# A hybrid decoder layer: the first adaLN weights loaded in two halves of features, with half contractions of two gate tiles and the norm statistics of all chunks between them

## The chip, the cores and the metric

The kernel runs on one core of a Trainium2 chip. The metric is the device time of one execution in microseconds; lower is better. It is one layer of one inference step in float32, launched once.

## The reference

Only the part around the change matters here. Tokens are the columns: 1024 of a prompt and 8 x 4 of samples, 1056 in all; the model has 1024 features, 8 blocks of 128 (called k below).

```python
mod = silu(c) @ w_ada + b_ada      # -> shift1, scale1, gate1, shift2, scale2, gate2
xn  = RMSNorm(x) * (1 + scale1) + shift1
h, B, C, q, k, v, gate_conv, gate_att = split(xn @ w_in)
...
x = x + gate1 * ((sigmoid(gate_conv) * conv_out + sigmoid(gate_att) * attn_out) @ w_o)
```

`w_ada` has 6144 columns; the first 2048 give shift1 and scale1. Behind these lines come a gated convolution, a dilated attention with caches, and an MLP; the change does not touch them.

## The kernel before

The program is a Python class, `Trunk`, that issues the instructions of every engine in an order written out by hand. Each engine works through its own instructions in that order and waits on semaphores where it needs another engine's result.

**Number format.** A float32 product is computed as three passes of a rounded format: each operand is split into a high part (a cast on ScalarE, ACT) and a low part (a subtraction on VectorE, DVE, or GpSimd, POOL), and `gemm` (L365) issues high x high, high x low and low x high for every k: 24 matmuls for a tile of 128 outputs and a chunk of columns. `prep_to` (L185) does this split for a weight tile, `load_to` (L175) loads its raw form into one of 8 weight buffers.

**Chunks and tiles.** The 1056 columns are worked on in 3 chunks of 352 (`CH`). The first four output tiles are gate tiles (w_in tiles 60 to 63), computed with `gemm` by `plain_tiles` (L290): the chunks in turn with tiles 0, 1 and 2, then tile 3. Behind them follow pairs of tiles in a scheme with fewer products (`pair_job`, L243), which needs the products of weights that `products` (L211) makes on ACT and DVE, and sums of the normalised input that `sums` (L325) makes on DVE and POOL.

**The start** (`start`, L429). SP issues the loads in this order: x of chunk 0, `w_ada` for k = 0 to 3, x of chunk 1, `w_ada` for k = 4 to 7, gate weight 0, x of chunk 2, gate weight 1. A load of `w_ada` is a tile of 128 x 1024. Meanwhile:

- `bias_rows` (L604) makes three rows of relative bias on PE and DVE.
- `stats(ch)` (L479) squares the 8 blocks of a chunk on ACT, adds them up on POOL, sums over partitions with a matmul on a matrix of ones, makes the reciprocal root (ACT, then DVE: L387 to L396) and multiplies the 8 blocks by it on DVE (L497). It runs for chunks 0 and 1, with the first four k's of `ada` between them.
- `ada(0)` (L565) computes the 2048 columns as four strips of 32 rows: for each k four matmuls with the same stationary operand (32 columns) at four column positions of the array, each streaming 512 columns. The result is copied, turned by four transposes, and the bias is added; `mod_mul` (L550) makes the scale.
- `apply(ch)` (L501) goes with `modulate` (L398) over the 8 blocks: scale and shift (DVE for even k, ACT for odd k; for chunk 2 two narrow DVE instructions per k besides, L420, for the sample columns), the cast to the high part (ACT) and the low part (DVE for even k, POOL for odd k). Chunk 0 is done at the start.

**Behind the start** a background queue (`bg`) is served in small portions by `slot` (L104) while the gate tiles are issued: `rest` (L509) does `apply(1)`, the statistics of chunk 2 and `apply(2)`; then come `sums` and `bias_spread`. `need` (L137) drains the queue as far as a tile requires. `evac` (L89) copies a finished gate tile out of PSUM, on ACT or DVE in turn.

PSUM banks: three of kind "g", two of kind "s", one each of the others.

Of the kernel before, what the change touches and what calls it, by code (L numbers as in the profile page):

```python
# [17 lines left out]
P = 128  # L18
# [31 lines left out]
class Trunk:  # L50
# [261 lines left out]

    def operand(self, n, k, p):
# [84 lines left out]
    def modulate(self, c, src, r, mul_t, add_t, out, y):  # L398
        nc = self.nc
        n = NPC2 if c == 2 else CH  # L400
        for step in range(KD + 3):
            k = step - 3
            if 0 <= k:
                hi, lo = out(k)
                eng = nc.gpsimd if k % 2 else nc.vector
                eng.tensor_tensor(out=lo, in0=y(k), in1=hi.bitcast(F32), op=ALU.subtract)  # L406
            k = step - 2
            if 0 <= k < KD:
                nc.scalar.copy(out(k)[0], y(k))
            k = step - 1  # L410
            if 0 <= k < KD:
# [11 lines left out]
            if k < KD and r is not None:  # L423
# [5 lines left out]
    def start(self):  # L429
# [20 lines left out]
        wada = self.ada_loads(0, range(4))  # L450
        load_x(1)
        wada.update(self.ada_loads(0, range(4, KD)))
        self.load_to(0)
        load_x(2)
        self.load_to(1)
# [23 lines left out]
        def stats(ch):  # L479
            s = slice(ch * CH, (ch + 1) * CH)  # L480
            acc = None
            for k in range(KD):
                sq = self.chunk("sq")
                nc.scalar.activation(sq, xp[k][:, s], AF.Square)
                if acc is None:
                    acc = sq
                else:
                    nc.gpsimd.tensor_tensor(out=acc, in0=acc, in1=sq, op=ALU.add)
                if k % 2:
                    yield 300  # L490
            ss = self.bank("ada")[:, :CH]
            nc.tensor.matmul(ss, self.ones, acc, start=True, stop=True)
            tmp, r0, r = self.chunk("ln"), self.chunk("r0"), self.chunk("r")
            self.neg_rstd(r, ss, tmp, r0, eps[:, 0:1], 1024 * EPS)
            yield 300
            for k in range(KD):
                nc.vector.tensor_tensor(out=xp[k][:, s], in0=xp[k][:, s], in1=r, op=ALU.mult)  # L497
                if k % 2:
                    yield 300

        def apply(ch):  # L501
            s = slice(ch * CH, (ch + 1) * CH)
            for k, _ in enumerate(self.modulate(ch, None, None, self.mul1, self.add1,
                                                lambda k: (self.xh[k][:, s], self.xl[k][:, s]),
                                                lambda k: xp[k][:, s])):
                if k % 2:
                    yield 300

        def rest():  # L509
            st2 = stats(2)  # L510
            for i, c in enumerate(apply(1)):
                yield c
                if i < KD // 2:
                    yield next(st2)
            self.ready.add(("xn", 1))
            yield None
            yield None
            yield from st2
            yield from apply(2)
            self.ready.add(("xn", 2))  # L520
            nc.scalar.preload_act_table_set("sigmoid_and_others")

        def run(g, n=1 << 30):
            for _ in range(n):
# [1433 lines left out]
```

## Time and profile before

| | |
|---|---|
| median of 3 runs (lowest to highest) | 2165.97 us (2165.32 to 2166.7) |
| the profiled execution | 2163.8 us |
| its span | 2162.0 us |
| mean granted TensorE clock | 0.979 |
| busy: PE, DVE, ACT, POOL | 94%, 65%, 46%, 36% of the span |
| bytes moved | 325.84 MB, mean 151 GB/s |

The profile is of one execution. Its times count from the start of the span, 0 to 2162 us; the execution's own time is 1.8 us more. PE is TensorE's matmul, PEld its weight load, SPq the queue in which SP issues transfers. A granted clock of 1.00 is 2.4 GHz, 0.50 is 1.2 GHz. An entry "[2.54 <-DVE wlo L197]" says that the engine was idle for 2.54 us before the instruction and that DVE's line 197 ended the wait. A float32 matmul without the split shows as two records.

### The profile page before, as it was taken

How to read it: one execution, taken by the hardware profiler on the slowest of the kernel's cores; microseconds unless marked ns; L12 is line 12 of the kernel's file. 1: busy time of each engine (PE TensorE's matmuls, PEld its weight loads, DVE VectorE, ACT ScalarE, POOL GpSimd, SP SyncE). 2: the span in 40 equal slices, each digit the busy share in tenths (PEclk: the TensorE clock that was granted, in tenths of full speed). 3: DMA queues.
4: the chain of work that ended last, by engine and by line, in shares of the span. 5: the costliest groups of instructions: out<-in, count | busy, mean ns of one | idle time of the engine just before them, and what ended most of it. 6: DMA issues, size and time to landing. Idle time of an engine off the chain costs nothing.

```text
span 2162.0 us, 38832 instructions
## 1 busy us (share of the span) xinstructions
PE 2021.7 (94%) x15092; PEld 1907.2 (88%) x15092; DVE 1404.3 (65%) x2935; ACT 989.3 (46%) x2193; POOL 782.6 (36%) x553
## 2 busy tenths in 40 slices
PE   5899999999999999999997989988999999999998
PEld 2799999889899888888886878988999999999998
DVE  4846665435656666556676676378444447999997
ACT  4522223335566556555554322355555556433332
POOL 3645555320111111100011114235233235788785
PEclk8899999999999999999998999999999999999999
DMA  7242221764122445333246774432347729555542
GB/s 284 71 136 62 79 70 35 250 212 148 45 69 74 144 149 167 104 114 116 67 125 199 238 233 145 162 125 88 130 158 274 256 90 350 203 202 198 197 158 102
DMA packets 138096, 325.84 MB, mean 151 GB/s; under 512 B 34232, under 2 KB 77880, under 8 KB 136888
## 3 DMA queue, kind: packets, MB, share of 16 engines
q1 hardware_dynamic: 137480, 323.17, 44.5%
q8 instruction: 118, 1.93, 0.4%
q14 instruction: 66, 0.54, 0.1%
q10 hardware_dynamic: 432, 0.20, 0.0%
HBM read 270.48 MB, written 112.07 MB: 177 GB/s over the span
## 4 chain that ended last, share of the span: by engine, by line
PE 56%; DVE 23%; ACT 5%; issue 3%; DMA 3%; POOL 2%; SPq 0%; DVEq 0%; POOLq 0%; ACTq 0%
PE ps_g L377 23%; DVE acc L1721 5%; DVE wprod L162 5%; PE ps_g L264 4%; PE ps_s L264 4%; PE ps_g L266 4%; PE ps_s L266 4%; PE ps_s L265 4%; PE ps_g L265 4%; DVE hl L1573 1%; DVE wlo L197 1%; ACT S L987 1%; PE ps_o L1015 1%; DVE S L979 1%; PE ps_s L973 1%
## 5 line engine op out<-in xcount | busy, mean ns | idle before, releaser
L162 DVE TENSOR_TENSOR wprod<-wraw,wprod 128x512 fp32r<-128x512 f32 x276 | 270.1, 981 | 173.9 <-ACT wprod L158 173.8
L377 PE MATMUL ps_g<-xh,whi 128*128 128x352 f32 x1056 | 356.6, 338 | 12.8 <-ACT whi L193 6.5
L377 PE MATMUL ps_g<-xh,wlo 128*128 128x352 f32 x1056 | 346.3, 328 | 5.6 <-DVE wlo L197 5.4
L377 PE MATMUL ps_g<-xl,whi 128*128 128x352 f32 x1056 | 346.6, 328 | 3.0 <-POOL xl L406 2.2
L377 PEld LDWEIGHTS ps_g<-xh,whi 128*128 128x128 f32 x1056 | 203.2, 192 | 35.6 <-issue 16.1
L158 ACT CAST wprod<-wraw 128x512 fp32r<-128x512 f32 x276 | 163.3, 618 | 151.0 <-DVE wprod L162 104.1
L377 PEld LDWEIGHTS ps_g<-xl,whi 128*128 128x128 f32 x1056 | 203.9, 193 | 5.9 <-POOL xl L406 4.0
L377 PEld LDWEIGHTS ps_g<-xh,wlo 128*128 128x128 f32 x1056 | 202.7, 192 | 7.2 <-DVE wlo L197 7.2
L197 DVE TENSOR_TENSOR wlo<-wraw,whi 128x512 fp32r<-128x512 f32 x184 | 130.0, 748 | 45.6 <-PE ps_g L377 25.4
L162 POOL TENSOR_TENSOR lo<-qn,hi 128x1024 fp32r<-128x1024 f32 x12 | 33.2, 2770 | 346.7 <-ACT hi L158 346.7
L277 POOL TENSOR_TENSOR ps_z<-ps_z,ps_s 128x264 f32<-128x264 f32 x64 | 60.3, 944 | 252.0 <-DVE ps_s L276 251.8
L264 PE MATMUL ps_s<-th,wprod 128*128 128x264 f32 x512 | 146.3, 286 | 1.7 <-DVE ps_s L276 1.7
L264 PE MATMUL ps_g<-th,wprod 128*128 128x264 f32 x512 | 146.9, 287 | 0.0
L266 PE MATMUL ps_g<-th,wprod 128*128 128x264 f32 x512 | 145.8, 285 | 0.0
L265 PE MATMUL ps_s<-tl,wprod 128*128 128x264 f32 x512 | 145.8, 285 | 0.0
L266 PE MATMUL ps_s<-th,wprod 128*128 128x264 f32 x512 | 145.7, 285 | 0.0
L265 PE MATMUL ps_g<-tl,wprod 128*128 128x264 f32 x512 | 145.5, 284 | 0.0
L987 ACT ACTIVATE S<-S,ng 128x128 f32<-128x128 f32 (+1 forms) x192 | 84.2, 441 | 124.7 <-DVE ng L982 122.8
L193 ACT CAST whi<-wraw 128x512 fp32r<-128x512 f32 x184 | 104.2, 619 | 32.1 <-DMA wraw<-in_w_conv_out 11.4
L264 PE MATMUL ps_g<-xh,wprod 128*128 128x264 f32 x384 | 110.6, 288 | 3.2 <-ACT wprod L158 3.2
L266 PE MATMUL ps_g<-xh,wprod 128*128 128x264 f32 x384 | 110.3, 287 | 3.5 <-DVE wprod L162 3.5
L264 PE MATMUL ps_s<-xh,wprod 128*128 128x264 f32 x384 | 109.9, 286 | 3.4 <-DVE ps_s L280 3.4
(383 smaller groups left out, 6448.3 us busy)
## 6 DMA issues: line engine op xcount, KB each, us to landing
wraw<-in_w_in SPq DMA_DIRECT2D x76, 512.0 KB, 4.1
wada<-in_w_ada SPq DMA_DIRECT2D x48, 512.0 KB, 5.6
hid_d<-hid SPq DMA_DIRECT2D x32, 528.0 KB, 2.9
wraw<-in_w_mlp_in SPq DMA_DIRECT2D x32, 512.0 KB, 6.1
wraw<-in_w_mlp_out SPq DMA_DIRECT2D x32, 512.0 KB, 3.9
hraw<-hid_d SPq DMA_DIRECT2D x56, 264.0 KB, 4.4
kv<-in_v SPq DMA_DIRECT2D x28, 512.0 KB, 5.6
wraw<-in_w_conv_out SPq DMA_DIRECT2D x24, 512.0 KB, 6.7
```

Of the source, the lines that this page charges most:

```text
L158: nc.scalar.copy(hi, src)
L162: eng.tensor_tensor(out=lo, in0=src, in1=hi.bitcast(F32), op=ALU.subtract)
L193: self.nc.scalar.copy(hi[:, s], w[:, s])
L197: self.nc.vector.tensor_tensor(out=lo[:, s], in0=w[:, s], in1=hi[:, s].bitcast(F32), op=ALU.subtract)
L264: nc.tensor.matmul(ps, hi, xh, start=(k == 0), stop=False)
L265: nc.tensor.matmul(ps, hi, xl, start=False, stop=False)
L266: nc.tensor.matmul(ps, lo, xh, start=False, stop=(k == 3))
L277: nc.gpsimd.tensor_tensor(out=z[p], in0=z[p], in1=s[p], op=ALU.add)
L377: self.nc.tensor.matmul(ps, a, x, start=(i == 0), stop=(i == n - 1))
L973: nc.tensor.matmul(ps[hh][:, 256 * i:256 * i + N], q[a][pr, q0:q0 + P], k[b][pr, k0:k0 + N], start=(x == 0), stop=(x == 2))
L987: nc.scalar.activation(s, s, AF.Exp, bias=ng[:, hh, i:i + 1], accum_out=sm[:, hh, i:i + 1])
L1721: nc.vector.tensor_tensor(out=a, in0=a, in1=ps, op=ALU.add)
```

## The change

The `w_ada` loads come in two halves of features. Half f holds the columns of blocks 4f to 4f + 3 of both shift1 and scale1, as tiles of 128 x 2 x 512, one per k. SP's order becomes: x of chunk 0, half 0 (8 loads), gate weight 0, x of chunk 1, gate weight 1, x of chunk 2, half 1 (8 loads), gate weights 2 and 3.

`ada_mm` issues two matmuls (strips f and 2 + f) per k and half. After half 0, blocks 0 to 3 of a chunk can be scaled and shifted, and `first(i, ch, 0)` issues their 12 matmuls, the upper half of the contraction, for gate tiles 0 and 1; the partial sums stay in six PSUM banks. The order is: statistics of chunk 0, weight 0, half 0, `apply(0, 0)`, tile 0; statistics of chunk 1, weight 1, tile 1, `apply(1, 0)`, four k's of half 1, tiles 0 and 1 of chunk 1; statistics of chunk 2, `apply(2, 0)`, the other four k's of half 1, tiles 0 and 1 of chunk 2; the result of half 1, `apply(0, 1)`. `first_tiles` then finishes tiles 0 and 1 chunk by chunk, with `apply(1, 1)` and `apply(2, 1)` from the background queue, and computes tiles 2 and 3 as before. In `stats` the adds are shared: even blocks on POOL, odd ones on DVE, and two matmuls on ones add the two sums.

```diff
--- before.py
+++ after.py
@@ -310,6 +310,30 @@
                 self.wt.pop(base + i)
             self.slot()
 
+    def first_tiles(self, consume):
+        for ch in range(NCH):
+            self.need(("xn", ch))
+            for i in range(2):
+                self.first(i, ch, 1)
+                self.slot()
+                consume(i, ch, self.banks.pop((i, ch)))
+                if ch == 2:
+                    self.wt.pop(i)
+            if ch:
+                self.prep_to(1 + ch, True)
+        for i in range(2, NG):
+            for ch in range(NCH):
+                s = slice(ch * CH, (ch + 1) * CH)
+                ps = self.bank("g")
+                self.gemm(ps[:, :CH], self.wt[i], range(KD), [(self.xh[k][:, s], self.xl[k][:, s]) for k in range(KD)])
+                consume(i, ch, ps)
+                if i == NG - 1:
+                    self.products_to(1 + ch)
+                if i == NG - 2 and ch == 0:
+                    self.load_to(NG)
+                self.slot()
+            self.wt.pop(i)
+
     def operand(self, n, k, p):
         if 2 <= n <= 5:
             i, t = ((0, 0), (1, 1), (0, 1), (1, 0))[n - 2]
@@ -395,20 +419,20 @@
         nc.vector.scalar_tensor_tensor(out=tmp, in0=ss, scalar=eps, in1=tmp, op0=ALU.add, op1=ALU.mult)
         nc.vector.scalar_tensor_tensor(out=out, in0=tmp, scalar=1.5, in1=r0, op0=ALU.subtract, op1=ALU.mult)
 
-    def modulate(self, c, src, r, mul_t, add_t, out, y):
+    def modulate(self, c, src, r, mul_t, add_t, out, y, k0=0, k1=KD):
         nc = self.nc
         n = NPC2 if c == 2 else CH
-        for step in range(KD + 3):
+        for step in range(k0, k1 + 3):
             k = step - 3
-            if 0 <= k:
+            if k0 <= k:
                 hi, lo = out(k)
                 eng = nc.gpsimd if k % 2 else nc.vector
                 eng.tensor_tensor(out=lo, in0=y(k), in1=hi.bitcast(F32), op=ALU.subtract)
             k = step - 2
-            if 0 <= k < KD:
+            if k0 <= k < k1:
                 nc.scalar.copy(out(k)[0], y(k))
             k = step - 1
-            if 0 <= k < KD:
+            if k0 <= k < k1:
                 w = y(k)
                 if k % 2:
                     nc.scalar.activation(w[:, :n], w[:, :n], AF.Identity, bias=add_t[:, k, 0:1], scale=mul_t[:, k, 0:1])
@@ -420,7 +444,7 @@
                         nc.vector.tensor_tensor(
                             out=v, in0=v, in1=tt[:, k, 1:9].unsqueeze(2).to_broadcast([P, NB, NT]), op=op)
             k = step
-            if k < KD and r is not None:
+            if k < k1 and r is not None:
                 nc.vector.tensor_tensor(out=y(k), in0=src(k), in1=r, op=ALU.mult)
             yield
 
@@ -447,12 +471,22 @@
         nc.scalar.dma_start(out=blk, in_=t["blk"])
         self.vec = vec = c.tile([P, 128], F32, name="vec")
         nc.scalar.dma_start(out=vec, in_=t["vec"])
-        wada = self.ada_loads(0, range(4))
+        wada = [[], []]
+
+        def load_ada(f):
+            for k in range(KD):
+                w = self.page("wada", (P, 2, 512))
+                nc.sync.dma_start(
+                    out=w, in_=t["w_ada"][k * P:(k + 1) * P, 0:2048].rearrange("p (a f n) -> p a f n", a=2, f=2)[:, :, f])
+                wada[f].append(w)
+
+        load_ada(0)
+        self.load_to(0)
         load_x(1)
-        wada.update(self.ada_loads(0, range(4, KD)))
-        self.load_to(0)
+        self.load_to(1)
         load_x(2)
-        self.load_to(1)
+        load_ada(1)
+        self.load_to(3)
         self.b_ada, self.g1, self.g2 = vec[:, 0:48], vec[:, 48:56], vec[:, 56:64]
         self.cw = vec[:, 64:88].rearrange("p (a k) -> p a k", a=3)
         eps = c.tile([P, 2], F32, name="eps")
@@ -478,79 +512,123 @@
 
         def stats(ch):
             s = slice(ch * CH, (ch + 1) * CH)
-            acc = None
+            acc = [None, None]
             for k in range(KD):
                 sq = self.chunk("sq")
                 nc.scalar.activation(sq, xp[k][:, s], AF.Square)
-                if acc is None:
-                    acc = sq
+                if acc[k % 2] is None:
+                    acc[k % 2] = sq
                 else:
-                    nc.gpsimd.tensor_tensor(out=acc, in0=acc, in1=sq, op=ALU.add)
-                if k % 2:
-                    yield 300
-            ss = self.bank("ada")[:, :CH]
-            nc.tensor.matmul(ss, self.ones, acc, start=True, stop=True)
+                    eng = nc.vector if k % 2 else nc.gpsimd
+                    eng.tensor_tensor(out=acc[k % 2], in0=acc[k % 2], in1=sq, op=ALU.add)
+            ss = self.bank("pt")[:, :CH]
+            for i in range(2):
+                nc.tensor.matmul(ss, self.ones, acc[i], start=(i == 0), stop=(i == 1))
+            del acc
             tmp, r0, r = self.chunk("ln"), self.chunk("r0"), self.chunk("r")
             self.neg_rstd(r, ss, tmp, r0, eps[:, 0:1], 1024 * EPS)
-            yield 300
             for k in range(KD):
                 nc.vector.tensor_tensor(out=xp[k][:, s], in0=xp[k][:, s], in1=r, op=ALU.mult)
-                if k % 2:
-                    yield 300
-
-        def apply(ch):
+
+        def apply(ch, f):
             s = slice(ch * CH, (ch + 1) * CH)
             for k, _ in enumerate(self.modulate(ch, None, None, self.mul1, self.add1,
                                                 lambda k: (self.xh[k][:, s], self.xl[k][:, s]),
-                                                lambda k: xp[k][:, s])):
+                                                lambda k: xp[k][:, s], 4 * f, 4 * f + 4)):
                 if k % 2:
                     yield 300
 
+        def run(g):
+            for _ in g:
+                pass
+
+        ada_ps = self.bank("ada")
+        ada_m = self.page("ada_m", (P, 512))
+        nc.gpsimd.memset(ada_m, 0.0)
+
+        def ada_mm(f, ks):
+            for k in ks:
+                for c in (f, 2 + f):
+                    nc.tensor.matmul(ada_ps[32 * c:32 * c + 32, :], self.cT[:, k, :], wada[f][k][:, c // 2],
+                                     start=(k == 0), stop=(k == KD - 1), tile_position=(0, 32 * c))
+
+        def ada_out(f):
+            nc.scalar.copy(ada_m[32 * f:32 * f + 32, :], ada_ps[32 * f:32 * f + 32, :])
+            c = 2 + f
+            nc.vector.tensor_copy(ada_m[32 * c:32 * c + 32, :], ada_ps[32 * c:32 * c + 32, :])
+            tr = self.bank("pt")
+            for b in range(4):
+                self.turn(tr[:, b * P:(b + 1) * P], ada_m[:, b * P:(b + 1) * P], self.ident)
+            v = tr.rearrange("p (b c x) -> p c b x", b=4, x=32)
+            for c in (f, 2 + f):
+                nc.vector.tensor_tensor(
+                    out=self.modT[:, 4 * c:4 * c + 4, :], in0=v[:, c, :, 0:9],
+                    in1=self.b_ada[:, 4 * c:4 * c + 4].unsqueeze(2).to_broadcast([P, 4, 9]), op=ALU.add)
+            h = slice(4 * f, 4 * f + 4)
+            self.mod_mul(self.mul1[:, h], 8 + 4 * f, self.g1[:, h])
+
+        def operands():
+            for k in range(4):
+                for v, n in ((self.xh, "xh"), (self.xl, "xl")):
+                    v.append(self.page(n, dt=F32R))
+
+        banks = {}
+
+        def first(i, ch, f):
+            if not f:
+                banks[i, ch] = self.bank("g" if i == 0 else ("s", "ss", "o")[ch])[:, :CH]
+            s = slice(ch * CH, (ch + 1) * CH)
+            hi, lo = self.wt[i]
+            for k in range(4 * f, 4 * f + 4):
+                b = slice(k * P, (k + 1) * P)
+                for x, (a, v) in enumerate(((hi, self.xh), (hi, self.xl), (lo, self.xh))):
+                    nc.tensor.matmul(banks[i, ch], a[:, b], v[k][:, s], start=(k == 0 and x == 0), stop=(k == KD - 1 and x == 2))
+
         def rest():
-            st2 = stats(2)
-            for i, c in enumerate(apply(1)):
-                yield c
-                if i < KD // 2:
-                    yield next(st2)
-            self.ready.add(("xn", 1))
-            yield None
-            yield None
-            yield from st2
-            yield from apply(2)
-            self.ready.add(("xn", 2))
+            for ch in (1, 2):
+                yield from apply(ch, 1)
+                self.ready.add(("xn", ch))
             nc.scalar.preload_act_table_set("sigmoid_and_others")
 
-        def run(g, n=1 << 30):
-            for _ in range(n):
-                if next(g, self) is self:
-                    return
-
         self.bias_rows(*rel)
-        run(stats(0))
-        ada = self.ada(0, wada)
-        run(ada, 1)
-        st1 = stats(1)
-        run(st1)
-        run(ada)
-        self.mod_mul(self.mul1, 8, self.g1)
+        stats(0)
+        self.prep_to(0)
+        ada_mm(0, range(KD))
         self.add1 = self.modT[:, 0:8, :]
-        del wada, ada
-        self.xh = [self.page("xh", dt=F32R) for _ in range(KD)]
-        self.xl = [self.page("xl", dt=F32R) for _ in range(KD)]
-        self.prep_to(0, True)
-        ap0 = apply(0)
-        run(ap0, 1)
-        self.flush_later()
-        run(ap0)
+        ada_out(0)
+        self.xh, self.xl = [], []
+        wada[0] = None
+        operands()
+        run(apply(0, 0))
+        first(0, 0, 0)
+        stats(1)
+        self.prep_to(1)
+        first(1, 0, 0)
+        run(apply(1, 0))
+        ada_mm(1, range(4))
+        first(0, 1, 0)
+        first(1, 1, 0)
+        stats(2)
+        run(apply(2, 0))
+        ada_mm(1, range(4, KD))
+        first(0, 2, 0)
+        first(1, 2, 0)
+        ada_out(1)
+        wada[1] = ada_ps = None
+        del ada_m
+        operands()
+        run(apply(0, 1))
         self.ready.add(("xn", 0))
         self.bg.append(rest())
         self.bg.append(self.sums())
         self.bg.append(self.bias_spread())
+        self.first, self.banks = first, banks
 
     def mod_mul(self, out, t0, g):
         nc = self.nc
-        nc.vector.tensor_scalar(out, self.modT[:, t0:t0 + 8, :], -32.0, -32.0, op0=ALU.mult, op1=ALU.add)
-        nc.vector.tensor_tensor(out=out, in0=out, in1=g.unsqueeze(2).to_broadcast([P, KD, 9]), op=ALU.mult)
+        n = out.shape[1]
+        nc.vector.tensor_scalar(out, self.modT[:, t0:t0 + n, :], -32.0, -32.0, op0=ALU.mult, op1=ALU.add)
+        nc.vector.tensor_tensor(out=out, in0=out, in1=g.unsqueeze(2).to_broadcast([P, n, 9]), op=ALU.mult)
 
     def ada_loads(self, r, ks):
         ws = {}
@@ -562,20 +640,17 @@
                 ws[k, h] = w
         return ws
 
-    def ada(self, r, ws=None):
-        nc = self.nc
-        acc = self.bank("o" if r else "ada")
+    def ada(self, r):
+        nc = self.nc
+        acc = self.bank("o")
         for k in range(KD):
-            if r:
-                ws = None
-                ws = self.ada_loads(r, [k])
-                yield 4
+            ws = None
+            ws = self.ada_loads(r, [k])
+            yield 4
             for c in range(4):
                 nc.tensor.matmul(
                     acc[32 * c:32 * c + 32, :], self.cT[:, k, :], ws[k, c // 2][:, (c % 2) * 512:(c % 2 + 1) * 512],
                     start=(k == 0), stop=(k == KD - 1), tile_position=(0, 32 * c))
-            if k % 4 == 3 and not r:
-                yield 1
         ws = None
         m = self.page("ada_m", (P, 512))
         nc.vector.tensor_copy(m, acc)
@@ -1318,7 +1393,7 @@
         self.rate = 700.0
 
         st = {}
-        self.plain_tiles(0, "xn", lambda i, ch, ps: self.gate(i, ch, ps, st.setdefault(i, {})))
+        self.first_tiles(lambda i, ch, ps: self.gate(i, ch, ps, st.setdefault(i, {})))
         self.last_prod = 7 * sum(len(j) == 2 for j in jobs[NG:])
         ji = NG
         while len(jobs[ji]) == 2:
```

## Rows read from the trace of the kernel before

**Rows 1.** The page, busy us of each engine (share of the span) xinstructions.
```profile
PE 2021.7 (94%) x15092; PEld 1907.2 (88%) x15092; DVE 1404.3 (65%) x2935; ACT 989.3 (46%) x2193; POOL 782.6 (36%) x553
```

**Rows 2.** Windows: stretch, length, each engine's busy us (xinstructions), PEclk, DMA share, GB/s.
```profile
42.64:110.78 68.14, 56.76 (x290) 52.88 (x291) 58.16 (x83) 41.09 (x72) 40.80 (x31) 0.86 0.23 76
0.00:42.64 42.64, 17.33 (x78) 4.00 (x79) 17.44 (x40) 14.71 (x29) 13.81 (x18) 0.90 0.96 346
```

**Rows 3.** Timeline of PE: start, us, engine, line, out<-in, xcount [idle <-releaser].
```profile
17.19 1.54 PE L492 MATMUL ps_s<-sq,ones 128*128 128x352 f32 x2 [2.15 <-POOL sq L488]
18.66 4.71 PE L574 MATMUL ps_s<-wada,cT 128*32 128x512 f32 x32
...
42.64 0.66 PE L377 MATMUL ps_g<-xh,whi 128*128 128x352 f32 x1 [2.11 <-ACT xh L409]
...
110.78 0.28 PE L264 MATMUL ps_g<-xh,wprod 128*128 128x264 f32 x1
```

**Rows 4.** Windows within the gate stage, columns as in rows 2.
```profile
64.00:78.00 14.00, 14.00 (x87) 13.84 (x86) 10.90 (x33) 6.39 (x13) 3.40 (x5) 1.00 0.00 1
96.00:102.00 6.00, 5.34 (x18) 5.34 (x19) 6.00 (x6) 3.75 (x5) 2.98 (x3) 0.50 0.68 212
```

**Rows 5.** Windows of the transfers at the start, columns as in rows 2.
```profile
22.00:24.00 2.00, 1.37 (x16) 0.15 (x8) 2.00 (x5) 1.65 (x4) 0.58 (x1) 1.00 1.08 367
...
28.00:30.00 2.00, 0.00 (x0) 0.00 (x0) 0.24 (x1) 0.00 (x0) 1.92 (x2) 0.50 1.04 416
...
44.00:46.00 2.00, 2.00 (x7) 1.62 (x8) 1.09 (x3) 1.85 (x4) 1.10 (x2) 0.50 0.09 35
```

**Rows 6.** Timeline of PE's weight loads for w_ada, columns as in rows 3.
```profile
19.52 0.20 PEld L574 LDWEIGHTS ps_s<-wada,cT 128*32 128x32 f32 x4 [0.66 <-issue]
20.37 0.20 PEld L574 LDWEIGHTS ps_s<-wada,cT 128*32 128x32 f32 x4 [0.66 <-issue]
...
21.91 0.12 PEld L574 LDWEIGHTS ps_s<-wada,cT 128*32 128x32 f32 x4 [0.31 <-issue]
22.34 0.12 PEld L574 LDWEIGHTS ps_s<-wada,cT 128*32 128x32 f32 x4 [0.31 <-issue]
```

**Rows 7.** Timeline of DVE and POOL from the w_ada result on.
```profile
39.13 0.69 DVE L581 COPY ada_m<-ps_s 128x512 f32<-128x512 f32 x1
...
41.61 0.46 DVE L416 TENSOR_SCALAR x<-x,mul,modT 128x352 f32<-128x352 f32 x1
41.99 1.28 DVE L197 TENSOR_TENSOR wlo<-wraw,whi 128x512 fp32r<-128x512 f32 x2
...
45.78 0.94 POOL L406 TENSOR_TENSOR xl<-x,xh 128x352 fp32r<-128x352 f32 x1 [0.90 <-ACT xh L409]
```

**Rows 8.** Timeline of ACT, POOL and DVE: statistics, of chunk 1 but for the first row.
```profile
10.20 6.94 POOL L488 TENSOR_TENSOR sq<-sq 128x352 f32<-128x352 f32 x7 [9.76 <-ACT sq L484]
...
22.34 3.86 ACT L484 ACTIVATE sq<-x 128x352 f32<-128x352 f32 x8 [1.90 <-DMA x<-in_xT]
...
23.42 7.61 POOL L488 TENSOR_TENSOR sq<-sq 128x352 f32<-128x352 f32 x7 [6.28 <-ACT sq L484]
...
35.65 3.57 DVE L497 TENSOR_TENSOR x<-x,r 128x352 f32<-128x352 f32 x8
```

**Rows 9.** Lines by form, DVE, gate stage: xcount | busy us, mean ns | idle.
```profile
L420 DVE TENSOR_TENSOR x<-x,modT 128x32 f32<-128x32 f32 x8 | 3.5, 431 | 0.3
```

**Rows 10.** Timeline of DVE: the first sums, the first weight product.
```profile
79.35 2.05 DVE L335 TENSOR_TENSOR x<-x 128x528 f32<-128x528 f32 x2
...
106.97 0.68 DVE L162 TENSOR_TENSOR wprod<-wraw,wprod 128x512 fp32r<-128x512 f32 x1
```

**Rows 11.** Timeline of PE: the longest late waits of the gate stage, and one behind it.
```profile
93.20 0.63 PE L377 MATMUL ps_g<-xh,whi 128*128 128x352 f32 x1 [3.34 <-DVE graw L99]
...
96.66 0.66 PE L377 MATMUL ps_g<-xh,wlo 128*128 128x352 f32 x1 [2.54 <-DVE wlo L197]
...
133.04 0.39 PE L264 MATMUL ps_g<-xh,wprod 128*128 128x264 f32 x1 [1.66 <-ACT wprod L158]
```

## Prediction, written before the changed kernel was run

> **What bounds the kernel now.** I read the busy line first: TensorE (PE) is busy 94% of the span [rows 1], so a gain or a loss has to come from time in which PE does not run at its pace. The change touches only the start and the four gate tiles, so the next view is the table by stretches, cut where the first gate matmul and the first paired matmul begin [rows 2, 3]: 42.64 us pass before the first gate matmul, and the gate stage takes 68.14. Undisturbed, PE issues a 352-column matmul every 14.00/87 = 0.161 us at a granted clock of 1.00 (2.4 GHz), and every 5.34/18 = 0.297 us at 0.50 (1.2 GHz) [rows 4]. The stage has 4 tiles x 3 chunks x 24 = 288 matmuls, 46.4 us at the fast pace, so 21.8 us of it are waits and half clock. VectorE (DVE) is busy for 58.16 of the 68.14 us [rows 2]. So there are two prizes: the front, in which PE is nearly idle, and DVE's late work. The change goes for the first.
>
> The front looks bound by transfers: the DMA share is 0.96 [rows 2], and they have ended by 46 us [rows 5]. The reader should ask whether the new order of work keeps up with them.
>
> **The change part by part.** The engines work in program order, so I walk the new order. Times are us from the span's start.
>
> *Transfers.* The same bytes come in another order, with gate weights 2 and 3 sooner; SP issues as many DMAs, and the stores of the bias rows, moved behind more loads, are read only much later. With the second half of w_ada behind x, all has landed by about 46. Its rows are now 2 KB, not 4. The bounds: nothing, and the rate of the stretch in which x (rows of 1.4 KB) arrives, 367 GB/s for 416 [rows 5], on 8.4 MB: 22.9 us for 20.2, +2.7. I take nothing, because the second half is first used after 52 and last after 60 in the walk below; without that cover it costs the 2.7.
>
> *First half of w_ada.* The statistics of chunk 0 end near 18.7 as now [rows 3]: the adds are shared by POOL and DVE, but DVE first does the bias rows, and a second matmul on ones is added. Now 4 k's with four column strips take 4.71 [rows 3]; the weight loads of a pass come in fours, 0.85 apart at the low and 0.43 at the high clock [rows 6]. A k has two passes, so 1.70 or 0.86, with four strips side by side. The change issues two strips per k, hence 16 such steps in place of 8. Bounds for the first 8: 4.7 if a step costs by its matmuls, 13.6 at the low clock; I take 2 x 4.71 = 9.4, since a pass streams the same 512 columns however many strips stand beside it. It ends at 28.1.
>
> By the Trainium skill, "TensorEngine Tiling (Array Packing)", Key Properties, tiles work independently and in parallel; by that rule half the strips save nothing per step, which speaks against this change, and the forecast stands as below, whereas with cost by matmul it would be 4.7 lower. The fours of rows 6 agree with it; no row has a step of two strips.
>
> *First scale and shift.* From the copy of the w_ada result to the first modulation 2.48 pass now [rows 7], so 30.6. The half apply (4 k's): now POOL can start on k = 3 at 45.78, so ScalarE (ACT) is free 4.2 after 41.61, with 1.28 of weight low parts on DVE in between [rows 7]; I take 3.5 to ACT free and 4.5 to the end of POOL's low part. ACT is free at 34.1.
>
> *The link.* ACT reaches the squares of chunk 1 only then. Now its statistics take from 22.34 to 39.22 = 16.9, and POOL's adds end at 31.03 [rows 8]. With the adds shared, the last sum is there 1.0 after the squares (3.86), 4.9 after the start in place of 8.7: -3.8. The second matmul on ones costs +1.2 (0.6 to 1.54, what the present one takes [rows 3]). So a link is 14.3: squares, sums, ones, reciprocal root, 8 normalising instructions. The zero fill of a page on POOL lies in the 9.76 in which POOL has nothing to do [rows 8]; without them it would cost one add, 1.0. Chunk 1 is normalised at 48.4; weight 1's low parts, 1.3 [rows 7], make it 49.7; ACT is free at 53.2, and the low part of k = 3 is there at 54.2.
>
> Chunk 2 would follow at 53.2 + 14.3 = 67.5. But its matmul on ones stands on PE behind 12 matmuls of tile 1 (to 52), four w_ada steps (4.7, to 56.7) and 24 matmuls of the chunk-1 halves (3.9 to 7.1): to 60.6 or 63.8, whereas the sums are ready at 58.1. That is +2.5 to +5.7; I take 2.5, the full clock, since these follow one another closely: 70.0. The half apply has 8 narrow per-sample instructions besides, of 0.43 or less [rows 9] and partly beside other work: 5.2, so 75.2. Then come on PE the last 15 matmuls of the chunk-2 halves, 2.4 to 4.5, taken as 3.4, and behind them the transposes of the second half, with their adds 1.5 (1.8 now [rows 7], with twice as many adds). **The upper half of chunk 0 starts at A = 80.1.**
>
> *What is left on PE.* 72 of 288 matmuls are done. The next 12 go at the pace of the half apply, 5.0; the other 204 x 0.161 = 32.8. For waits behind DVE I take 4, between 0 and 10. The stage ends at 80.1 + 5.0 + 32.8 + 4.0 = 121.9, against 110.78 now [rows 3]: **+11.1**. The second prize is not won either: DVE can start the sums only when all second halves are applied, at A + 4.5 + 4.5 + 5.2 = A + 14.2. From their first instruction to the first weight product 28.3 pass now (79.35 to 107.65 [rows 10]), so the product comes at 122.6. PE and DVE give the same end.
>
> *Behind it* nothing waits on the wall clock: PE goes on at 94%, so the shift stays. The longest such waits now are 3.34 and 2.54 in the gate tiles, and 1.66 for pair weights at 133 [rows 11]; the last may move by a few us either way.
>
> The profiled execution took 2163.8; 2163.8 + 11.1 = 2174.9. The median of the three runs, 2165.97, is 2.2 above it: 2177.
>
> **The rivals.**
> 1. *Everything at its lower end* (no difference). Strips by matmul -4.7, PE's queue -2.5, the 15 matmuls -1.0, waits -4: by PE 2165. DVE does not wait less: A is 71.9, and A + 14.2 + 28.3 = 114.4, +3.6, gives 2170. So 2165 to 2170; that it needs every bound at once speaks against it.
> 2. *The transfers set the front* (faster). Then A is near 50 (landed by 46, last w_ada steps, 2.5 of output), the stage ends at 50 + 41.8 = 92, and the time is 2158 if half of those 19 us are kept, 2147 if all. It decides from A = 110.8 - 41.8 = 69. The DMA share of 0.96 speaks for it. ACT's order speaks against it: 34.1 plus two links is 62.7, with two half applies 71.
> 3. *Half clock through the front* (slower still). Rows 4 and 11 show PE at a granted 0.50 after it had waited; in the new front it works in bursts with waits between. Cost: the first half of w_ada at 13.6 for 9.4, +4.2; four later steps at 6.8 for 4.7, +2.1; 24 matmuls +3.2; 15 matmuls +1.1; in sum 10.6, so 2188. The close queue on PE from 49 to 61 speaks against the middle two.
>
> The Trainium skill, "TensorE: Matmul & The Clock Gate", HAM oscillation, says that bursts with long waits between them each start throttled again. The low clock from 96 to 102, behind two waits, agrees; that is rival 3, with its time.
>
> **How the numbers follow.** Forecast 0.60, rival 1 0.15, rival 2 0.10, rival 3 0.15. A measurement of this kernel tells 0.2%, about 4.3 us, from no change. The forecast and rival 3 are slower by more: 0.75; rival 1 is the same: 0.15; rival 2 is faster: 0.10. The range runs from rival 1's floor, 2165, to rival 3, 2188; it leaves out rival 2 and a tail in which the waits add to rival 3.
>
> **What would show it.** In the changed profile: the first gate matmul near 32, ten us sooner than now; w_ada steps of two strips as long as those of four; ACT idle between the squares of a chunk and its logarithm; the second half of chunk 0's apply at about 80, long after the last w_ada transfer; the first paired matmul near 122, with DVE busy without a break before it. If the upper half starts before 69, the forecast is wrong in sign. If the stage ends at 122 and the total is no longer, something behind it gave the time back, and the wait for pair weights is the place to look.

## The result, and the profile after

The changed kernel takes 2181.57 us (median of 4 runs, 2177.85 to 2183.83) against 2165.7 (median of 4) for the kernel before on the same chip. The ratio is 1.0069, 95% interval 1.0052 to 1.0087: 11 to 19 us slower. The forecast of 2177 had the sign right and the range held the time. But one large term of the sum was missing, and the trace shows it at once.

The page's busy line of the changed kernel, which answers to [rows 1]: PE is busy 15 us longer and still holds only 93% of the span. 6.8 of the 15 are the w_ada steps: 7.91, 4.69 and 3.63 for twice 4.71 [rows 3].

```profile
PE 2036.4 (93%) x15102; PEld 1916.0 (88%) x15102; DVE 1401.3 (64%) x2947; ACT 989.8 (45%) x2195; POOL 769.1 (35%) x542
```

The windows of the changed kernel, columns as in [rows 2]: the front up to the first gate matmul, the gate stage, and two stretches at the end of the transfers.

```profile
0.00:30.99 30.99, 15.83 (x46) 3.60 (x46) 11.88 (x32) 9.97 (x19) 3.51 (x8) 1.00 0.95 325
30.99:132.95 101.96, 71.34 (x333) 57.65 (x333) 63.92 (x102) 46.27 (x84) 37.03 (x30) 0.77 0.29 101
...
40.00:44.00 4.00, 0.00 (x0) 0.00 (x0) 0.00 (x0) 0.00 (x0) 0.00 (x0) 0.50 1.05 402
44.00:48.00 4.00, 0.95 (x2) 0.50 (x2) 0.00 (x0) 0.00 (x0) 1.90 (x3) 0.50 0.14 54
```

The front is shorter by 11.65 (42.64 to 30.99), the stage longer by 33.82 (68.14 to 101.96). So the first paired matmul comes 22.17 later, where +11.1 was forecast. The third row is the one to stop at: for 4 us no compute engine does anything at all, and only transfers run. In a stage that is bound by a chain of engines one of them should be busy; here none is, so what they wait for is no engine's work, and a transfer is the first thing to look for.

The timeline of PE in the changed kernel, columns as in [rows 3], shows the steps of the walk and the hole:

```profile
19.12 7.91 PE L552 MATMUL ps_s<-wada,cT 128*32 128x512 f32 x32
...
30.99 0.57 PE L585 MATMUL ps_g<-xh,whi 128*128 128x352 f32 x1 [1.85 <-ACT xh L433]
...
47.01 0.66 PE L585 MATMUL ps_g<-xl,whi 128*128 128x352 f32 x1 [11.77 <-POOL xl L430]
...
49.90 2.72 PE L526 MATMUL ps_pt<-sq,ones 128*128 128x352 f32 x4 [1.94 <-POOL sq L523]
...
108.44 0.43 PE L401 MATMUL ps_g<-xh,wlo 128*128 128x352 f32 x1 [2.99 <-DVE wlo L197]
...
132.95 0.29 PE L264 MATMUL ps_g<-xh,wprod 128*128 128x264 f32 x1
```

PE waits 11.77 for POOL's low part of block 3. The timelines of POOL, ACT, DVE and SP say why. Each is followed from the instruction that waited to the one that released it:

```profile
46.03 0.92 POOL L430 TENSOR_TENSOR xl<-x,xh 128x352 fp32r<-128x352 f32 x1 [12.97 <-DMA rows<-rw]
46.91 2.93 POOL L523 TENSOR_TENSOR sq<-sq 128x352 f32<-128x352 f32 x3
...
52.71 0.55 ACT L413 ACTIVATE ln<-ps_pt,eps 128x352 f32<-128x352 f32 x1 [16.08 <-PE ps_pt L526]
...
54.42 0.52 DVE L419 SCALAR_TENSOR_TENSOR ln<-ps_pt,ln 128x352 f32<-128x352 f32 x1 [17.23 <-ACT ln L415]
...
29.05 4.66 SPq L479 DMA_DIRECT2D wada<-in_w_ada  x8
33.76 1.64 SPq L180 DMA_DIRECT2D wraw<-in_w_in  x2
36.47 2.95 SPq L688 DMA_DIRECT2D rows<-rw  x3
```

POOL has nothing to read from the transfer `rows<-rw` that it waits for. It waits to write: the page for the low part is one that held a bias row (`rw`), and the store of that row, 12 KB, had not been done. SP issues the three stores behind half 1 of w_ada and two gate weights, and the transfers work these off until about 45: the page comes free at 46.03. POOL's three adds for chunk 1 stand behind it, then PE's sum, ACT's logarithm, DVE's normalising. One late page holds up the queues of all four compute engines for some 12 us (of the waits of 16.08 and 17.23 on ACT and DVE, 4.28 and 4.20 are left in e1, where the page is free).

In time the stores were not moved back. The timeline of SP in the kernel before has them at 38.44, with two gate weights fewer ahead of them (what these two add was not tried):

```profile
38.44 1.22 SPq L613 DMA_DIRECT2D rows<-rw  x3
```

What the change moved is the next use of the page. POOL asks for it at 33.06 (46.03 less 12.97); before, its low part of block 3 came at 45.78 [rows 7], and no wait for a store shows there.

By the Trainium skill, "DMA: Bandwidth & Descriptors", Queues, rings and completion order, each DMA engine takes its descriptors in ring order. The trace agrees: POOL is released when the loads ahead of the small store are through (DMA share 1.05 from 40 to 44, 0.14 from 44 to 48).

Further on, DVE's timeline has the start of the upper half (A in the forecast), the first sums and the first weight product:

```profile
88.97 0.46 DVE L440 TENSOR_SCALAR x<-x,mul,modT 128x352 f32<-128x352 f32 x1
...
100.96 0.70 DVE L359 TENSOR_TENSOR x<-x 128x528 f32<-128x528 f32 x1
...
130.08 0.68 DVE L162 TENSOR_TENSOR wprod<-wraw,wprod 128x512 fp32r<-128x512 f32 x1
```

**What was given back.** ACT loads an activation table when the paired tiles are done; that is a mark of their end in every trace. The timeline of ACT has it in the kernel before, and in the changed one:

```profile
512.76 1.28 ACT L1335 ACT_TABLE_LOAD   x1
```

```profile
530.49 1.28 ACT L1410 ACT_TABLE_LOAD   x1
```

The paired stage went from 401.98 (512.76 less 110.78) to 397.54, so 4.44 of the 22.17 came back. More than half of it is the wait for pair weights [rows 11]. Windows of 5 us at the same distance behind the start of the paired stage, 20.0, before and after:

```profile
130.78:135.78 5.00, 3.12 (x23) 2.69 (x23) 2.72 (x7) 1.14 (x2) 1.43 (x1) 1.00 0.97 333
```

```profile
152.95:157.95 5.00, 5.00 (x44) 5.00 (x43) 4.28 (x8) 1.42 (x4) 4.09 (x3) 1.00 0.77 306
```

PE issued 21 matmuls fewer before, at 5.00/44 = 0.114 each 2.4 us. SP issues the loads of those weights 14.0 after the stage's end before, 11.4 after it now. What is left of the shift is 17.7, within the interval of 11 to 19.

### The profile page after: what moved, and what is told of

Same layout as the page of the kernel before. It is cut to its first block, busy times and chain, and to the rows that moved or that the text cites. A ratio compares the mean times of both kernels' runs of the same rounds, so it can differ in the third digit from the quotient of the medians.

```text
span 2182.0 us, 38856 instructions
## 1 busy us (share of the span) xinstructions
PE 2036.4 (93%) x15102; PEld 1916.0 (88%) x15102; DVE 1401.3 (64%) x2947; ACT 989.8 (45%) x2195; POOL 769.1 (35%) x542
## 4 chain that ended last, share of the span: by engine, by line
PE 60%; DVE 22%; ACT 6%; DMA 5%; issue 4%; POOL 3%; SPq 0%; DVEq 0%; POOLq 0%; ACTq 0%
PE ps_g L401 24%; PE ps_g L264 4%; PE ps_s L264 4%; PE ps_g L266 4%; PE ps_s L265 4%; PE ps_s L266 4%; PE ps_g L265 4%; DVE wprod L162 4%; DVE acc L1796 4%; DVE wlo L197 1%; ACT S L1062 1%; DVE S L1054 1%; DVE hl L1648 1%; PE ps_s L1048 1%; PE ps_o L1090 1%
## 5 line engine op out<-in xcount | busy, mean ns | idle before, releaser
L401 PE MATMUL ps_g<-xh,whi 128*128 128x352 f32 x1008 | 339.4, 337 | 4.8 <-ACT whi L193 4.3
L401 PE MATMUL ps_g<-xh,wlo 128*128 128x352 f32 x1008 | 329.8, 327 | 5.2 <-DVE wlo L197 5.1
L401 PE MATMUL ps_g<-xl,whi 128*128 128x352 f32 x1008 | 329.5, 327 | 1.0 <-POOL xl L430 0.7
L401 PEld LDWEIGHTS ps_g<-xh,whi 128*128 128x128 f32 x1008 | 193.3, 192 | 25.7 <-issue 16.1
L401 PEld LDWEIGHTS ps_g<-xh,wlo 128*128 128x128 f32 x1008 | 193.0, 191 | 6.4 <-DVE wlo L197 6.4
L401 PEld LDWEIGHTS ps_g<-xl,whi 128*128 128x128 f32 x1008 | 194.0, 192 | 2.0 <-POOL xl L430 0.9
```

The source lines that it names most:

```text
L401: self.nc.tensor.matmul(ps, a, x, start=(i == 0), stop=(i == n - 1))
```

## The experiments

Each kernel was timed beside the kernel before on the same chip: e1, e2 and e3 together (before 2164.35), e4 and e5 together (2163.37), e6 (2163.73). None leaves out a part of the computation.

**e1: the bias rows in buffers of their own.** The changed kernel, with one line changed, so that the stores hold no page that chunk 0 wants.

```diff
-            rw = self.page("rw", (8, 384))
+            rw = self.half("rw", (8, 384))
```

> The changed kernel, but the three bias rows lie in buffers of their own, not in pages that the operands of chunk 0 take over. Theory (POOL's low part of k = 3 waits 12.97 us for a page whose store stands on SP behind the second half of w_ada): that low part comes at 33 to 34 in place of 46.0, the upper half of chunk 0 starts at 76 to 80 in place of 88.97, the gate stage ends at 120 to 124 in place of 132.9, and the time falls by 9 to 12 us, to 2169 to 2175; what is left against the kernel before is the price of the serial links. Rival (DVE's late work absorbs the wait): the stage ends less than 3 us sooner, 2178 to 2182.

2171.31 us (9 runs), ratio 1.0038 (1.0023 to 1.0052). Timelines of POOL, PE and DVE in e1:

```profile
34.56 0.94 POOL L430 TENSOR_TENSOR xl<-x,xh 128x352 fp32r<-128x352 f32 x1 [0.56 <-ACT xh L433]
...
18.78 9.20 PE L552 MATMUL ps_s<-wada,cT 128*32 128x512 f32 x32
...
97.20 0.43 PE L401 MATMUL ps_g<-xh,wlo 128*128 128x352 f32 x1 [3.05 <-DVE wlo L197]
...
77.71 0.46 DVE L440 TENSOR_SCALAR x<-x,mul,modT 128x352 f32<-128x352 f32 x1
...
118.84 0.68 DVE L162 TENSOR_TENSOR wprod<-wraw,wprod 128x512 fp32r<-128x512 f32 x1
...
121.70 0.29 PE L264 MATMUL ps_g<-xh,wprod 128*128 128x264 f32 x1
```

POOL begins the low part of block 3 at 34.56 (33 to 34 expected), no longer at 46.03. The stage ends at 121.70, 11.25 sooner, though SP issues the stores when it did (36.58). The page was the wait. By the medians the time fell by 10.3, by the two ratios to the kernel before by 6.7; their intervals meet at 1.0052. e1 also shows the rest of the forecast undisturbed: A 77.71 for 80.1, the stage's end 121.70 for 121.9. That the end is met so closely is luck: A comes 2.4 sooner than forecast, and what is left behind it takes 2.2 longer (see below).

**e2: the statistics of all chunks in front, w_ada whole.** The kernel before, with the other part of the change alone: adds shared by DVE and POOL, chunk 2's x loaded ahead of the second four k's, gate weight 0 behind them, and chunk 2's statistics ahead of their matmuls.

```diff
         wada = self.ada_loads(0, range(4))
         load_x(1)
-        wada.update(self.ada_loads(0, range(4, KD)))
-        self.load_to(0)
         load_x(2)
+        wada.update(self.ada_loads(0, range(4, KD)))
...
-        st1 = stats(1)
-        run(st1)
+        run(stats(1))
+        run(stats(2))
         run(ada)
```

> One part alone: the kernel before, with the statistics of all three chunks in the front (adds shared by POOL and DVE, x of chunk 2 loaded ahead of the second four k's of w_ada), w_ada not split. Theory (the front is then bound by transfers, 1.44 MB of x in front of w_ada cost 3.7 us, DVE and POOL save a chunk's statistics in the gate stage): first gate matmul 3 to 4 us later, at 46; first weight product on DVE 4 to 8 us sooner than 107; stage end 106 to 112; 2160 to 2167. Rival a (DVE alone sets the stage): 2157 to 2160. Rival b (PE's own pace sets the stage): the later front shows in full, 2168 to 2170.

2163.22 us (10 runs), ratio 0.9991 (0.9978 to 1.0004): no difference. Timelines of PE and DVE in e2:

```profile
37.56 1.54 PE L493 MATMUL ps_pt<-sq,ones 128*128 128x352 f32 x2 [6.32 <-POOL sq L488]
...
41.81 1.54 PE L493 MATMUL ps_pt<-sq,ones 128*128 128x352 f32 x2 [2.71 <-DVE sq L488]
43.28 4.71 PE L569 MATMUL ps_s<-wada,cT 128*32 128x512 f32 x32
...
53.32 0.66 PE L377 MATMUL ps_g<-xh,whi 128*128 128x352 f32 x1 [2.11 <-ACT xh L409]
...
108.42 0.69 DVE L162 TENSOR_TENSOR wprod<-wraw,wprod 128x512 fp32r<-128x512 f32 x1 [2.69 <-ACT wprod L158]
...
114.95 0.28 PE L264 MATMUL ps_g<-xh,wprod 128*128 128x264 f32 x1
```

I had expected the first gate matmul at 46. It came at 53.32, because the last four k's of w_ada stand on PE behind two sums over ones that wait for POOL's and DVE's adds (37.56, 41.81). The first weight product is 1.45 later than before [rows 10], not 4 to 8 sooner; that it loses so little of the 10.68 of the front is because the work put in front is missing behind it. The stage ends 4.17 later, at 114.95, where 106 to 112 was expected. The time lies in the expected range only because the paired stage, whose weights SP issues 3.55 behind the stage's end in place of 14.0, gives 4.20 back. So statistics in front of an undivided w_ada neither gain nor lose. What they cost between the half applies, where the changed kernel has them, e2 does not show; e3 does.

**e3: the statistics of the next chunk ahead of the half apply.** e1, with squares, adds and the sum over ones split from the normalising, and issued one chunk early, so that a link of the chain no longer begins when the apply before it is over. The first four w_ada steps of half 1 also move, behind the chunk-1 halves.

```diff
+        ss = squares(1)
         run(apply(0, 0))
-        first(0, 0, 0)
-        stats(1)
+        norm(1, ss)
         self.prep_to(1)
-        first(1, 0, 0)
+        first(0, 0, 0)
+        ss = squares(2)
         run(apply(1, 0))
-        ada_mm(1, range(4))
+        first(1, 0, 0)
+        norm(2, ss)
...
-        stats(2)
+        ada_mm(1, range(4))
         run(apply(2, 0))
```

> e1_rw_own with the order of issue changed: squares and sums of the next chunk are issued ahead of the half apply of the present one, and the four w_ada steps behind the chunk-1 halves. Theory (the serial links of squares, sums, ones, root, normalising and half apply set the front): the upper half of chunk 0 starts 8 to 10 us sooner than in e1_rw_own, at 68 to 72, the stage ends at 111 to 115, 2162 to 2167. Rival (PE at half clock or DVE behind it sets the front, not the order on ACT): within 3 us of e1_rw_own.

2162.19 us (10 runs), ratio 0.9997 (0.9987 to 1.0006), the same as before. Timelines of DVE and PE in e3:

```profile
70.10 0.46 DVE L440 TENSOR_SCALAR x<-x,mul,modT 128x352 f32<-128x352 f32 x1
...
87.75 3.51 DVE L197 TENSOR_TENSOR wlo<-wraw,whi 128x512 fp32r<-128x512 f32 x2
...
111.27 0.68 DVE L162 TENSOR_TENSOR wprod<-wraw,wprod 128x512 fp32r<-128x512 f32 x1
...
89.58 0.43 PE L401 MATMUL ps_g<-xh,wlo 128*128 128x352 f32 x1 [2.78 <-DVE wlo L197]
...
112.56 0.29 PE L264 MATMUL ps_g<-xh,wprod 128*128 128x264 f32 x1
```

A falls by 7.6 against e1 (8 to 10 expected), the stage's end by 9.1 to 112.56. So the order of the links was what the second half of the loss was made of; what the squares and what the moved w_ada steps give of it was not tried apart. The 1.5 by which the end gains more than A is PE's clock: behind the wait for weight 2 the last 142 matmuls take 22.98, in e1 24.50, where twelve of them go 0.29 apart (granted clock 1.00 and 0.93). With both mended, the change costs nothing, and gains nothing.

**e4: the second half as early as its transfers allow.** e3, with all eight steps of half 1 and the upper half of chunk 0 behind chunk 0's first half, and chunk 2 applied whole.

```diff
-        ss = squares(2)
-        run(apply(1, 0))
...
-        ada_mm(1, range(4))
-        run(apply(2, 0))
-        ada_mm(1, range(4, KD))
...
+        acc = squares(2)
+        ada_mm(1, range(KD))
         ada_out(1)
...
+        ss = ones_mm(2, acc)
...
         run(apply(0, 1))
+        run(apply(1, 0))
...
+        run(apply(1, 1))
+        norm(2, ss)
```

> The kernel of e3_sums_ahead with all eight w_ada steps of the second half, its result and the upper half of chunk 0 taken right behind chunk 0's first half and the squares of chunk 2, and with chunk 2 applied whole. My theory (the front is a chain on ScalarE, VectorE and POOL that sets the start of the upper half, A, and DVE's 30 us behind the last apply set the end of the stage): A falls from 70.1 to about 52, since the second half of w_ada has landed by 46; but the chain's end, the last apply of chunk 2, moves by only some 3 to 5, so that the first weight product stands at 105 to 108, the stage ends at 107 to 111 and the time is 2157 to 2162. Rival (A itself sets the end of the stage, by the matmuls left on PE behind it): the stage ends some 18 sooner than in e3_sums_ahead, near 95, and the time is 2145 to 2150. Second rival (the four transposes and the result of the second half, taken early, hold up ScalarE for chunk 1): the stage ends at 113 or later and the time is 2163 or more.

2160.37 us (12 runs), ratio 0.9982 (0.9974 to 0.9991). Timelines of DVE and PE in e4:

```profile
51.07 0.47 DVE L442 TENSOR_SCALAR x<-x,mul,modT 128x352 f32<-128x352 f32 x1
...
77.11 1.32 DVE L361 TENSOR_TENSOR x<-x 128x528 f32<-128x528 f32 x2
...
84.61 3.55 DVE L197 TENSOR_TENSOR wlo<-wraw,whi 128x512 fp32r<-128x512 f32 x2
...
106.61 0.68 DVE L162 TENSOR_TENSOR wprod<-wraw,wprod 128x512 fp32r<-128x512 f32 x1
...
79.27 0.66 PE L597 MATMUL ps_g<-xl,whi 128*128 128x352 f32 x1 [0.77 <-POOL xl L432]
...
86.48 0.43 PE L403 MATMUL ps_g<-xh,wlo 128*128 128x352 f32 x1 [0.29 <-DVE wlo L197]
...
109.45 0.29 PE L264 MATMUL ps_g<-xh,wprod 128*128 128x264 f32 x1
```

A falls by 19.0, the stage's end by 3.1, as my theory had it. An early start of the upper half is worth little by itself: PE's matmuls still need the last operands of chunk 2, and DVE's sums, which come behind these, begin at 77.11 for 82.09 in e3. A is now near 50, as in rival 2 of the prediction, but this is no test of that rival's rule, end = A + 41.8: it has 72 of the 288 matmuls done at A, and here only 12 are, with chunks 1 and 2 still to be scaled and shifted.

**e5: the split of weight 2 out of the late chain.** e3, with one line more ahead of the copies of the second result.

```diff
         ada_mm(1, range(4, KD))
...
+        self.prep_to(2)
         ada_out(1)
```

> The kernel of e3_sums_ahead with the split of weight 2 into its parts (two DVE instructions) ahead of the copies of the second half of the w_ada result, where DVE was idle from 62.5 to 69. My theory (DVE's chain from A to the first weight product sets the end of the stage, and the split took 3.5 of it beside POOL's work): the first product comes 2 to 3.5 sooner, at 108 to 109.5, the stage ends at 109 to 111 and the time is 2159 to 2163. Rival (PE's matmuls set the end, DVE has room): the stage ends within 1 of 112.6 and the time is that of e3_sums_ahead, 2162, within 1.

2159.71 us (11 runs), ratio 0.9984 (0.9976 to 0.9993). Timelines of DVE and PE in e5:

```profile
63.21 1.61 DVE L197 TENSOR_TENSOR wlo<-wraw,whi 128x512 fp32r<-128x512 f32 x2 [0.76 <-ACT whi L193]
...
109.56 0.68 DVE L162 TENSOR_TENSOR wprod<-wraw,wprod 128x512 fp32r<-128x512 f32 x1
...
109.50 0.29 PE L264 MATMUL ps_g<-xh,wprod 128*128 128x264 f32 x1
```

Time and end are as expected, but not for my reason. The product came only 1.71 sooner, short of 2 to 3.5; the stage's end moved by 3.06, to before the product. What moved it is PE's wait of 2.78 for the low part of weight 2 (89.58 in e3), which is gone. From that wait on PE is busy without a break to the stage's end, in e3 as in the changed kernel (from 108.44); in e5 its trace shows no wait from 74.86 to 109.50. So PE's own matmuls set the end, and DVE takes part through the waits that it puts into them, not through the first product.

**e6: e4 with the split of weight 2 early.** Its high part on ACT behind the second result, its low part on DVE ahead of chunk 2's normalising.

```diff
         ada_out(1)
+        self.prep_to(2, lazy=True)
+        _, low2 = self.later.pop()
...
         run(apply(1, 1))
+        low2()
         norm(2, ss)
```

> The kernel of e4_half1_early with weight 2 split early as in e5_low2_front: its high part on ScalarE behind the second result of w_ada, its low part on DVE in the 1.95 in which DVE waits for the statistics of chunk 2, instead of the 3.55 that it takes at 84.61 beside POOL. In e4_half1_early the first weight product stood at 106.61 on DVE, but the stage ended 2.84 later, at 109.45, and PE was busy without a break from 90 on. Theory (from here PE's own matmuls set the end, DVE no longer): the first product comes 2 to 3.5 sooner, at 103 to 105, the stage ends within 1 of 109.5 and the time is 2159 to 2162, that of e4_half1_early within 1. Rival (DVE still sets it): the stage ends 2 to 3.5 sooner, at 106 to 107.5, and the time is 2156.5 to 2158.5.

2156.31 us (12 runs), ratio 0.997 (0.996 to 0.998): 4 to 9 us faster than the kernel before. Timelines of DVE and PE in e6:

```profile
61.72 2.04 DVE L197 TENSOR_TENSOR wlo<-wraw,whi 128x512 fp32r<-128x512 f32 x2
...
105.45 0.68 DVE L162 TENSOR_TENSOR wprod<-wraw,wprod 128x512 fp32r<-128x512 f32 x1
...
109.25 0.29 PE L264 MATMUL ps_g<-xh,wprod 128*128 128x264 f32 x1
```

The stage ends 0.20 sooner than in e4, within 1 as the theory says: in e4 PE waited only 0.29 for weight 2's low part (86.48), so there was no more to win. The product came 1.16 sooner, not 2 to 3.5, because the split on DVE also pushed the normalising back by 0.45 (63.75 for 63.30), and the next two subtractions on DVE (85.06, 87.80), which now stood beside POOL's adds, took 2.38 and 1.96 for 1.25 each in e4. The time, 2156.31, lies where the rival put it, though, and the stage's end does not: of the 4.06 between the medians of e4 and e6 (2.6 by their ratios, on two chips) the stage's end explains 0.2 and the paired stage 0.7. The intervals of e4 and e6 overlap; what the rest is, if it is more than the spread of the runs, is left open.

All kernels side by side: A, the end of the gate stage, the end of the paired stage (the table load) and how much later that is than before, beside the ratio's interval times 2165.

| kernel | A | stage ends | pairs end | pairs, later | time, later (95%) |
|---|---|---|---|---|---|
| before | - | 110.78 | 512.76 | 0 | 0 |
| changed | 88.97 | 132.95 | 530.49 | +17.7 | +11.3 to +18.8 |
| e1 | 77.71 | 121.70 | 520.06 | +7.3 | +5.0 to +11.3 |
| e2 | - | 114.95 | 512.73 | 0.0 | -4.8 to +0.9 |
| e3 | 70.10 | 112.56 | 511.97 | -0.8 | -2.8 to +1.3 |
| e4 | 51.07 | 109.45 | 507.78 | -5.0 | -5.6 to -1.9 |
| e5 | 69.81 | 109.50 | 509.53 | -3.2 | -5.2 to -1.5 |
| e6 | 51.51 | 109.25 | 506.89 | -5.9 | -8.7 to -4.3 |

In each row one trace's end of the paired stage lies within the interval of the times. So what happens up to there is enough to account for the verdicts, as far as one trace of each kernel can say.

## Why the prediction was right, and where it was wrong

- **The step that failed:** "the stores of the bias rows, moved behind more loads, are read only much later", costed at nothing. I asked who reads the stored rows. The question was who wants the buffer that is being stored. Its page went to chunk 0's low part of block 3, and POOL waited 12.97 for it. It was not the store that came later (SP issues it at 36.47, before at 38.44) but the use of the page that came sooner, at 33.06 for 45.78, ahead of the store. e1 prices the step: 11.25 at the stage's end.
- **The first half of w_ada** was taken at 9.4. It took 7.91 in the changed kernel, 9.20 in e1. Half the strips saved nothing per pass: the changed kernel's weight loads for two strips begin 0.43 apart (21.71, 22.14), with slower ones 0.86 apart ahead of them (19.97, 20.83), like the fours of [rows 6]. The difference is how many of the slow gaps there are, two in the changed kernel and five in e1. I called the slow ones the low clock, but the granted clock reads 1.00 in those stretches (18 to 20 before, 19 to 21 in the changed kernel); only their pace says so. The first gate matmul came at 30.99 where the text said near 32.
- **The link** was taken at 14.3 and chunk 1's normalised blocks at 48.4. In e1 the squares begin at 34.39 and the normalising ends at 48.33: 13.9. Chunk 2 follows at 68.47 (70.0 forecast), A at 77.71 (80.1).
- **What is left on PE** was 41.8 behind A; it is 44.0 in the changed kernel (88.97 to 132.95) and in e1 (77.71 to 121.70). The 2.2 are not the waits behind DVE: the allowance of 4 was ample, with 3.05 in e1 (97.20). The first 12 matmuls took 5.8 for 5.0, and the other 204 took 35.1 without that wait, for 32.8: of the stage's last 142, twelve go 0.29 apart, and others behind A do too. Half clock, which the sum left out here, is most of that 2.3. **DVE's chain** was A + 42.5; its product is complete at A + 41.8 in e1 and the changed kernel (start and 0.68). That the two give about the same end was right. e5 shows which of the two decides: PE.
- **Transfers with shorter rows** were costed at nothing, and cost little if anything: from 44 to 45 the DMA share is 0.53, before 0.18, and then it is near nothing in both.
- **"nothing waits on the wall clock", "the last may move by a few us either way":** 4.44 came back in the paired stage, more than half of it (2.4) the wait named there.
- **So the total** was near for two reasons that partly cancel: a missing +11, and -4.4 that was left at zero. By the profiled executions, +20.0 of span against the +11.1 forecast; by the medians +15.9. That the range holds the time is in part luck as well: its room above 2177 was meant for half clock, and a store's page used it.
- **Rival 1** (2165 to 2170) needed A at 71.9; e1's is 77.71. **Rival 2** (transfers set the front) is wrong in the changed kernel, where the front waits for a store, not for w_ada. e4 took A down to 51.07, and the stage still ended at 109.45, with most of chunks 1 and 2 behind A; an A near 50 with 72 matmuls done was not tried. The rival's 2158 is also a slip: half of 19 off 2166 is 2156.5. **Rival 3** (half clock): the granted clock of the stage is 0.77, for 0.86 before, and PE issues tile 1's first half 0.29 apart, at the low clock, behind its waits. But the w_ada steps took 7.91 and 4.69, not 13.6 and 6.8. In e1, with the clock at 0.81 in its stage, half clock is most of the 2.3 behind A named above, and A itself came 2.4 sooner than forecast.

## What to carry to other kernels

When work or a transfer is moved, ask for each store not only who reads what it writes, but which later operand takes over the buffer that it empties, and when: a store of 12 KB behind 5 MB of loads held four engines for 12 us once its page was wanted sooner. Look in the windows for a row in which no compute engine is busy, and follow it to the one transfer behind it. Work taken out of an idle front pays only if what sets the later stage's end moves too: here the last chunk's operands and PE's waits for a weight's low part. e5 gained by their order alone, with A where e3 had it; e4, with A 19 sooner, moved the stage's end hardly further than e5 did (3.11 and 3.06 against e3).

## What was not expected of the hardware

The low part of a weight (two subtractions of 128x512 on DVE) took 1.28 to 1.29 with POOL idle, but 3.51 in e3 at 87.75, while POOL added 128x528 blocks in the same stretch:

```profile
87.28 1.70 POOL L366 TENSOR_TENSOR x<-x 128x528 f32<-128x528 f32 x1 [0.64 <-DVE x L364]
88.94 1.77 POOL L360 TENSOR_TENSOR x<-x 128x528 f32<-128x528 f32 x1
```

By the Trainium skill, "Advanced Engine Details and Errata", GPSIMD Details, POOL shares a read and a write interface with DVE and conflicts with DVE instructions that have two inputs in SBUF. The trace agrees: the subtractions have two, and stretch 2.7 times. Moved to a stretch where POOL had little to do, the two took 1.61 (e5) and 2.04 (e6). No run took POOL's adds away, so the cause rests on the overlap in the traces.

Executions of one kernel spread by some 10 us (the kernel before from 2160.05 to 2170.11 in 24 runs). In the profiled ones part of it lies behind the paired stage, where the kernels issue the same instructions: from that table load to the next one ACT takes 837.3 (e1) to 843.6 (e4), and 839.7 in the kernel before. What causes it was not tried.
